# Reordering the projections of an RWKV-7 layer, moving its bonus product, and regrouping modulation and start-up loads

## The chip, the cores and the metric

The kernel runs on one core of one Trainium2 chip. The metric is the device time of one launch in microseconds (us). Three runs of the kernel before gave a median of 3932.47 us (3931.03 to 3934.02). The profile is of a fourth execution that took 3921.72 us.

## The reference, cut to what matters

The model has one RWKV-7 layer and one attention layer, each with a SwiGLU part, on 1024 prompt tokens and 8 x 16 sample tokens of width 1024, in float32. Only the first layer's mixing and the modulations matter here:

```
mod = silu(c) @ w_ada + b_ada                      # shift, scale, gate of each sublayer
h = rmsnorm(x) * (1 + scale) + shift;  xx = h_prev - h
xr, xw, xk, xv, xa, xg = h + xx * mix[0..5]
r, k, v = xr @ w_r, xk @ w_k, xv @ w_v
decay from sigmoid(w0 + tanh(xw @ w1) @ w2);  a = sigmoid(a0 + (xa @ a1) @ a2)
g = sigmoid(xg @ g1) @ g2                          # g1 is 1024 x 160: g1a 128 wide, g1b 32 wide
y, state = wkv7(r, decay, k, v, -kk, kk * a)       # a recurrence over tokens
y = groupnorm(y) * ln_w + ln_b + sum(r * k * r_k) * v    # the bonus
out = (y * g) @ w_o
```

## The kernel before, in words

**Arithmetic.** Most products split both operands into a high and a low float32r part and add three matmuls (`mm3`, line 257; `split`, line 253, is one ScalarE copy and one VectorE subtraction). A few small products are plain float32.

**Stages of the first layer.** The 1152 tokens are three blocks of 384 (`proj`, line 462). A block's projections are: `proj_h` (norm and modulation of h), the low-rank stage `proj_lora` (line 511: three first products wa1, g1a, g1b from the split h, then 24 second products of one or two short matmuls each, for w2, a2 and g2), `proj_k`, `proj_r`, `proj_v`, each eight output tiles (f) of 24 matmuls of 128 x 384. `mixed` (line 418) makes the 16 token-mixed tiles of an operand; they live in a ring `mix` of 17 slots, so the next operand's tiles come free as the last product of the one before consumes its own. Results go to DRAM (`spill`, `save`) and are read back by the recurrence.

**The recurrence.** A block has three windows of 128 tokens in two halves: six units. `inverses` (line 717) makes the small triangular inverses of a block's windows from the spilled kk and b: `win_first`, a solve on VectorE (`win_solve`, lines 792 to 796), four merge steps (`win_merge`), with DRAM round trips between. `win_prep` (line 729) loads and masks a unit's operands (rings XL, YL, BKT of three slots), `win_run` carries the state through the unit, `win_post` (line 962) normalises and gates. `windows` (line 1032) prepares two units ahead. Units of block b - 1 are alternated with the projections of block b, five steps to four (line 1100).

**The last stretch.** After the third block's projections the last six units (in the order 12, 13, 16, 14, 15, 17 of line 1113) alternate with `early`: 32 modulation steps, then the output projections of blocks 0 and 1; block 2's follows the units. Then come the SwiGLU part (its down projection carries the other 16 modulation units, `step(7)` in `begin`, line 1291) and the second layer.

**Modulations.** `ada_steps` (line 194): a unit of 512 columns has four loads of 512 KB, each followed by two plain float32 matmuls into two of four 32-row quarters of a bank, then a copy, four small matmuls and a bias add. The first four units are needed before the first block's h; their loads share the ring `raw` of three slots.

**What sets the order.** The building framework reorders each engine's instructions at build time: the order of the code is a priority, and what its own model of time holds ready, with a free slot, goes first. On the chip each engine and each DMA queue then keeps that fixed order.

Of the kernel before, what the change touches and what calls it, by code (L numbers as in the profile page):

```python
# [8 lines left out]
F32 = mybir.dt.float32  # L9
# [7 lines left out]
NB = 3  # L17
# [8 lines left out]
def _cst():  # L26
# [24 lines left out]
    add("qs", (p % 32)[:, None] == np.arange(16)[None, :])  # L51
    add("cen", np.eye(128) - (p[:, None] // 64 == p[None, :] // 64) / 64.0)
# [24 lines left out]
def prep(i):  # L77
# [38 lines left out]
    d["g2a"], d["g2b"] = g2[:128], np.concatenate([g2[128:]] * 3, 0)  # L116
# [24 lines left out]
class Trunk:  # L141
# [52 lines left out]
    def ada_steps(self, units, tag="aux", bufs=1):  # L194

        nc = self.nc
        for u in units:
            ps = self.bank(tag, bufs)
            for kp in range(4):
                w = self.rawtile()  # L200
                nc.sync.dma_start(w[:, :1024], self.a["wada"][u, kp])
                for j in range(2):
                    k = 2 * kp + j
                    q = 32 * (k % 4)
                    mm(nc, ps[q:q + 32, :], self.scT[:, k, :], w[:, j * 512:(j + 1) * 512], k < 4, k >= 4)
                if kp < 3:
                    yield
            sb = self.rawtile()[:, :512]
# [130 lines left out]
    def proj_open(self, ctx):  # L339
# [3 lines left out]
        self.nmix, self.nmr = 17, 2  # L343
# [8 lines left out]
    def lora_weights(self):  # L352

        nc, pp = self.nc, self.pp
        self.lw = {}
        for n, mixes, w in (("wa1", (1, 4), 64), ("g1a", (5,), 128), ("g1b", (5,), 32)):
            c = 8 * w * len(mixes)
            raw = pp.tile([128, 1024], F32, tag="raw", name=self.nm("raw"), bufs=self.nraw)
            nc.sync.dma_start(raw[:, :c], self.a[n])
            m = pp.tile([128, 1024], F32, tag="raw", name=self.nm("raw"), bufs=self.nraw)  # L360
            for j, i in enumerate(mixes):
                v = lambda t: t[:, :c].rearrange("p (k j w) -> p j k w", j=len(mixes), w=w)[:, j]
                nc.vector.tensor_tensor(v(m), v(raw), self.P(f"mix{i}").rearrange("p (k o) -> p k o", o=1).broadcast_to([128, 8, w]),
                                        ALU.mult)
            nc.vector.tensor_tensor(raw[:, :c], raw[:, :c], m[:, :c], ALU.subtract)
            self.lw[n] = []
            for t in (raw, m):
# [4 lines left out]
    def proj_h(self, b):  # L372
# [15 lines left out]
        for f in range(8):  # L388
            x = hb[:, f]
            if b == 0:  # L390
                if f % 4 == 0:
                    self.step(8)
# [69 lines left out]
    def proj(self, b):  # L462
# [17 lines left out]
        if b + 1 < NB:  # L480
            self.x = self.hsplit()
# [1378 lines left out]
```

## Time and profile before

| | |
|---|---|
| median of three runs | 3932.47 us |
| the profiled execution | 3921.72 us, span 3919.9 us |
| TensorE (PE) busy | 3594.0 us, 92% of the span, granted clock 0.928 on average |
| VectorE (DVE) busy | 2273.5 us, 58% |
| ScalarE (ACT) busy | 1588.3 us, 41% |
| GpSimd (POOL) busy | 632.7 us, 16% |
| DMA queue of SyncE (q1) | 375728 packets, 530.77 MB, 43.0% of 16 engines' span |
| chain that ended last | PE 64%, DMA 6%, DVE 5%, ACT 3% |

In the page's 40 slices (98 us each) PE is at 5 to 9 tenths and the clock at 6 to 9 tenths in the first 14 slices, that is, in the first layer's mixing; after that both are at 9 in nearly all slices. A busy TensorE is not TensorE at its peak: at a granted clock of 0.5 it is busy for twice as long with the same work.

### The profile page before, as it was taken

To read this page: it belongs to the slowest core of one execution; us is meant where nothing else is said; L and a number is where in the kernel's file an instruction comes from. 1 tells how busy PE (TensorE), PEld (TensorE's weight loads), DVE (VectorE), ACT (ScalarE), POOL (GpSimd) and SP (SyncE) were. 2 spreads that over 40 slices of the span, in tenths; PEclk is the share of its full clock that TensorE was granted. 3 is DMA by queue.
4 is the path that set the end of the run, shared out by engine and by line. 5 is a ranking of instruction groups with operands and counts; after the bars stand their busy time and mean duration, and the time that the engine had idled before them with its cause. 6 is when DMAs were issued, how large, how long until landed. Compare 5 with 4: busy or idle time off the path is not lost.

```text
span 3919.9 us, 71529 instructions
## 1 busy us (share of the span) xinstructions
PE 3594.0 (92%) x28214; PEld 3116.0 (79%) x28214; DVE 2273.5 (58%) x4259; ACT 1588.3 (41%) x2993; POOL 632.7 (16%) x569
## 2 busy tenths in 40 slices
PE   5788989999899789999999999898888799999999
PEld 3676777777568579999877888777677799999998
DVE  3667566564435765555355852566676765454567
ACT  4654546554223443333311254455554443333310
POOL 0000000000000265445000200100000365454000
PEclk8787889799689789999999999999999899999999
DMA  6774676576656422222655213255464422222522
GB/s 205 223 233 130 208 223 173 160 229 193 176 148 195 136 88 74 74 76 74 225 204 186 92 61 103 81 171 153 145 203 150 148 72 74 76 71 94 171 81 73
DMA packets 430208, 554.22 MB, mean 141 GB/s; under 512 B 128528, under 2 KB 297872, under 8 KB 425392
## 3 DMA queue, kind: packets, MB, share of 16 engines
q1 hardware_dynamic: 375728, 530.77, 43.0%
q10 hardware_dynamic: 54144, 18.89, 2.1%
q8 instruction: 222, 3.64, 0.4%
q14 instruction: 114, 0.93, 0.1%
HBM read 415.39 MB, written 134.12 MB: 140 GB/s over the span
## 4 chain that ended last, share of the span: by engine, by line
PE 64%; DMA 6%; DVE 5%; ACT 3%; issue 2%; POOL 1%; SPq 1%; ACTq 0%; DVEq 0%; POOLq 0%
PE S L138 31%; PE PT L138 15%; PE acc L138 8%; PE st L138 3%; PE O L138 2%; DVE h L255 1%; PE PT L1686 1%; PE aux L138 1%; PE G L138 1%; PE Y L138 1%; DMA rr<-sf_cs 1%; DMA mr<-yg 1%; ACT pts L1687 0%; ACT h L254 0%; DMA yg<-y 0%
## 5 line engine op out<-in xcount | busy, mean ns | idle before, releaser
L138 PE MATMUL S<-h,w 128*128 128x320 f32 (+1 forms) x4944 | 694.7, 299 | 17.8 <-DVE h L255 5.7
L138 PEld LDWEIGHTS S<-h,w 128*128 128x128 f32 x4944 | 674.8, 192 | 25.5 <-DVE h L255 10.0
L138 PE MATMUL acc<-mx,whi 128*128 128x384 f32 (+1 forms) x1824 | 527.0, 367 | 57.9 <-ACT whi L254 19.0
L138 PE MATMUL S<-h,wh 128*128 128x320 f32 (+1 forms) x2844 | 528.9, 337 | 13.5 <-DVE h L1056 8.1
L138 PEld LDWEIGHTS S<-h,wh 128*128 128x128 f32 x2844 | 454.4, 189 | 82.5 <-DVE h L1312 12.6
L138 PEld LDWEIGHTS acc<-mx,whi 128*128 128x128 f32 (+1 forms) x1824 | 344.1, 197 | 95.8 <-ACT whi L254 23.9
L254 ACT ACTIVATE w<-rq 128x512 fp32r<-128x512 f32 x308 | 192.0, 629 | 501.6 <-PE S L138 199.8
L255 DVE TENSOR_TENSOR w<-rq,w 128x512 fp32r<-128x512 f32 x308 | 271.4, 885 | 198.2 <-ACT w L254 197.5
L138 PE MATMUL PT<-h,w 128*128 128x320 f32 (+1 forms) x2448 | 353.3, 299 | 14.0 <-ACT w L254 6.4
L138 PEld LDWEIGHTS PT<-h,w 128*128 128x128 f32 x2448 | 335.7, 191 | 18.3 <-ACT w L254 6.8
L138 PE MATMUL acc<-mx,wlo 128*128 128x384 f32 (+1 forms) x912 | 328.3, 361 | 3.2 <-DVE wlo L255 3.2
L138 PE MATMUL PT<-h,wh 128*128 128x320 f32 (+1 forms) x1428 | 286.7, 344 | 6.7 <-DVE wh L255 3.9
L1245 POOL TENSOR_TENSOR t<-t,t 128x576 f32<-128x576 f32 (+1 forms) x132 | 215.0, 1629 | 412.4 <-ACT t L1252 296.0
L138 PEld LDWEIGHTS PT<-h,wh 128*128 128x128 f32 x1428 | 234.6, 191 | 42.0 <-DVE h L1312 6.9
L255 DVE TENSOR_TENSOR wlo<-raw,whi 128x1024 fp32r<-128x1024 f32 (+1 forms) x123 | 145.2, 1181 | 90.6 <-ACT whi L254 88.9
L138 PEld LDWEIGHTS acc<-mx,wlo 128*128 128x128 f32 (+1 forms) x912 | 179.5, 197 | 15.1 <-DVE wlo L255 5.9
L254 ACT ACTIVATE whi<-raw 128x1024 fp32r<-128x1024 f32 (+1 forms) x123 | 125.6, 1023 | 118.4 <-PE acc L138 93.4
L255 DVE TENSOR_TENSOR h<-h,h 128x1024 fp32r<-128x1024 f32 (+4 forms) x112 | 122.9, 1112 | 81.8 <-ACT h L254 67.3
L254 ACT ACTIVATE wh<-rq 128x512 fp32r<-128x512 f32 x124 | 74.6, 626 | 231.2 <-PE S L138 144.2
L254 ACT ACTIVATE h<-h 128x1024 fp32r<-128x1024 f32 (+4 forms) x112 | 103.2, 935 | 157.2 <-DMA h<-sd 113.4
L1312 DVE TENSOR_TENSOR h<-h,S 128x640 f32<-128x640 f32 (+1 forms) x150 | 112.1, 752 | 92.3 <-PE S L138 92.0
L1245 DVE TENSOR_TENSOR t<-S,t 128x576 f32<-128x576 f32 (+1 forms) x116 | 86.5, 745 | 132.7 <-PE S L138 132.5
(399 smaller groups left out, 5744.4 us busy)
## 6 DMA issues: line engine op xcount, KB each, us to landing
h<-in_wada SPq DMA_DIRECT2D x64, 512.0 KB, 6.1
raw<-in_wada SPq DMA_DIRECT2D x48, 512.0 KB, 4.4
rq<-in_wg SPq DMA_DIRECT2D x88, 256.0 KB, 2.6
rq<-in_wu SPq DMA_DIRECT2D x88, 256.0 KB, 2.6
rq<-in_wd SPq DMA_DIRECT2D x88, 256.0 KB, 3.0
kc<-in_ck SPq DMA_DIRECT2D x16, 1024.0 KB, 5.1
vc<-in_cv SPq DMA_DIRECT2D x16, 1024.0 KB, 5.9
sd<-t SPq DMA_DIRECT2D x88, 160.0 KB, 1.9
```

Source lines behind the costliest of these rows:

```text
L138: return nc.tensor.matmul(out, lhsT, rhs, start=start, stop=stop)
L254: self.nc.scalar.activation(hi, x, AF.Copy)
L255: self.nc.vector.tensor_tensor(lo, x, hi, ALU.subtract)
L1245: eng.tensor_tensor(out, x, y, ALU.add)
L1312: nc.vector.tensor_tensor(y, y, d, ALU.add)
L1686: nc.tensor.transpose(pt[:, j * 128:(j + 1) * 128], P[:, j * 128:(j + 1) * 128], self.C("ident"))
```

## The change

It reorders a block's projections to: first low-rank products, then v woven one to three with the second low-rank products, then k, the next block's h, and r with the inverses. It makes g1b a plain float32 product in four quarters, keeps the first block's low-rank weights in SBUF, does the bonus product per unit on GpSimd, moves two products of `proj_k` to GpSimd, regroups the modulations by four, gives the first modulation loads eight other tiles, shortens three rings of the recurrence from three to two and its look-ahead from two units to one. The core of the diff:

```diff
-    def ada_steps(self, units, tag="aux", bufs=1):
+    def ada_steps(self, units, tag="aux", bufs=1, tile=None):
...
-            for kp in range(4):
-                w = self.rawtile()
-                nc.sync.dma_start(w[:, :1024], self.a["wada"][u, kp])
-                for j in range(2):
-                    k = 2 * kp + j
-                    q = 32 * (k % 4)
-                    mm(nc, ps[q:q + 32, :], self.scT[:, k, :], w[:, j * 512:(j + 1) * 512], k < 4, k >= 4)
-                if kp < 3:
+            for h in range(2):
+                w = [(tile or self.rawtile)() for _ in range(2)]
+                for i in range(2):
+                    nc.sync.dma_start(w[i][:, :1024], self.a["wada"][u, 2 * h + i])
+                for q in range(4):
+                    mm(nc, ps[32 * q:32 * q + 32, :], self.scT[:, 4 * h + q, :], w[q // 2][:, q % 2 * 512:q % 2 * 512 + 512],
+                       h == 0, h == 1)
+                if h == 0:
                     yield
...
-        self.nmix, self.nmr = 17, 2
+        self.nmix, self.nmr = 18, 2
...
+    def lora_in(self, n):
+        c = 8 * self.LORA[n][1] * len(self.LORA[n][0])
+        if n not in self.lw:
+            ts = self.lora_weights(n)
+        else:
+            ts = [self.rawtile() for _ in range(2)]
+            for t, d in zip(ts, self.lw[n]):
+                self.nc.sync.dma_start(t[:, :c], d)
+        if n == "g1b":
+            return ts
...
     def proj(self, b):
         if b == 0:
-            self.ada = self.ada_steps((0, 2, 1, 3), "acc", 2)
+            self.lw = {}
+            ring = (f() for _ in range(3) for f in self.early)
+            self.ada = self.ada_steps((0, 2, 1, 3), "acc", 2, lambda: next(ring))
...
-            self.lora_weights()
...
-        x, k = self.x, self.mixed(2, b)
-        yield from self.proj_lora(b, *x)
+        x, v = self.x, self.mixed(3, b)
+        second = self.proj_lora(b, *x)
+        for _ in range(3):
+            yield next(second)
+        k = self.mixed(2, b)
+        yield from self.alternate(second, self.proj_v(b, *v), 3, 1)
         r = self.mixed(0, b)
         yield from self.proj_k(b, *k)
-        v = self.mixed(3, b)
-        yield from self.alternate(self.inverses(b), self.proj_r(b, *r))
         if b + 1 < NB:
             self.proj_h(b + 1)
-        yield from self.proj_v(b, *v)
-        if b + 1 < NB:
             self.x = self.hsplit()
+        yield from self.alternate(self.inverses(b), self.proj_r(b, *r))
...
-            self.save("bn", b, f, bn)
+            self.spill("bn", b, f, bn)
...
+        def narrow(n):
+            pw = self.bank("acc", 2)
+            W = self.lora_in(n)
+            for i in range(2):
+                for k in range(8):
+                    q = 32 * (k % 4)
+                    mm(nc, pw[q:q + 32, :TB], W[i][:, k * 32:k * 32 + 32], self.hgroups(self.hb[:, k])[i],
+                       i == 0 and k < 4, i == 1 and k >= 4)
+            u = self.ev("kk")
+            nc.scalar.activation(u, pw[:, :TB], AF.Copy)
+            mm(nc, pw[0:32, :TB], self.C("q4"), u, True, True)
+            return pw
...
-        pg = first("g1b", 32)
+        pg = narrow("g1b")
...
-            vv = self.ev("vv", 2)
-            self.load(vv, "bn", b, f)
             v = self.ev("e0", 4)
             nc.scalar.activation(v, pz[:, :TB], AF.Copy)
-            nc.vector.tensor_tensor(vv, vv, pz[:, :TB], ALU.mult)
-            nc.scalar.activation(vv, vv, AF.Identity, bias=self.P("lnb", f))
-            self.spill("v", b, f, vv)
+            self.spill("v", b, f, v)
...
-            nc.vector.tensor_tensor(ag, ag, iv, ALU.mult)
+            nc.gpsimd.tensor_tensor(ag, ag, iv, ALU.mult)
             self.spill("b", b, f, ag)
-            nc.vector.tensor_tensor(iv, iv, kp, ALU.mult)
+            nc.gpsimd.tensor_tensor(iv, iv, kp, ALU.mult)
...
+        self.early = [lambda: flat(self.wt("YL", [128, 2, 2, 4, 64], 2))] * 2 + \
...
-        ring, nr = (self.st, 1) if (w, hf) == (7, 1) and 1 else (self.wt, 3)
+        ring, nr = (self.st, 1) if (w, hf) == (7, 1) and 1 else (self.wt, 2)
...
+        bn = self.wt("bn", [128, 512], 1)
+        nc.sync.dma_start(bn.rearrange("p (f t) -> p f t", f=4), self.sp[b]["bn"][:, wi, fs, :])
+        nc.gpsimd.tensor_tensor(bv, bv, bn, ALU.mult)
...
-        nc.vector.tensor_tensor(y, y, gt, ALU.mult)
+        for f in range(4):
+            s = slice(f * 128, (f + 1) * 128)
+            nc.vector.scalar_tensor_tensor(y[:, s], y[:, s], self.P("lnb", 4 * hf + f), gt[:, s], ALU.add, ALU.mult)
...
-        n = 2
+        n = 1
...
-            for _ in range(32):
+            for _ in range(16):
...
-            self.step(7)
+            self.step(3)
```

## Rows read from the trace of the kernel before

**Rows 1.** Stretches: length, PE, PEld, DVE, ACT, POOL busy us, clock, DMA share, GB/s.
```profile
0.00:66.00 66.00, 25.94 (x99) 7.28 (x99) 22.43 (x54) 26.40 (x44) 1.29 (x8) 0.87 0.72 247
318.00:650.00 332.00, 298.39 (x3304) 246.59 (x3305) 214.99 (x472) 181.47 (x347) 4.89 (x19) 0.87 0.66 186
1006.00:1170.00 164.00, 143.16 (x1640) 94.53 (x1639) 68.57 (x179) 36.57 (x77) 0.00 (x0) 0.73 0.59 170
90.00:137.00 47.00, 40.25 (x130) 25.74 (x129) 23.63 (x33) 32.26 (x57) 0.19 (x1) 0.71 0.61 194
365.00:425.00 60.00, 52.99 (x636) 40.16 (x635) 33.76 (x64) 32.35 (x64) 0.29 (x1) 0.60 0.54 154
650.00:740.00 90.00, 83.55 (x808) 61.35 (x806) 54.12 (x114) 57.85 (x99) 0.00 (x0) 0.74 0.51 150
1890.00:2200.00 310.00, 310.00 (x1754) 238.59 (x1753) 166.46 (x258) 67.17 (x94) 4.60 (x3) 1.00 0.55 194
```

**Rows 2.** Timeline of the start: start us, us, engine, line, what, count, idle before.
```profile
17.49 26.37 SPq L201 DMA_DIRECT2D raw<-in_wada  x13
...
47.83 1.05 PE L138 MATMUL acc<-raw,scT 128*32 128x512 f32 x4 [0.22 <-DMA raw<-in_wada]
...
57.04 0.07 DVE L402 MEMSET hb<- 128x8 f32 x1
...
59.31 2.06 DVE L255 TENSOR_TENSOR mx<-hb,mx 128x408 fp32r<-128x408 f32 x4
...
61.74 14.91 SPq L247 DMA_DIRECT2D raw<-lw  x6
...
66.51 1.01 PE L138 MATMUL acc<-mx,whi 128*128 128x384 f32 x2 [15.86 <-ACT whi L254]
```

**Rows 3.** Timeline of PE in g1b's product of block 0.
```profile
88.72 0.34 PE L138 MATMUL acc<-mx,wlo 128*32 128x384 f32 x1
...
89.26 0.34 PE L138 MATMUL acc<-mx,wlo 128*32 128x384 f32 x1
```

**Rows 4.** Timeline of PE around modulation matmuls.
```profile
944.75 1.06 PE L138 MATMUL aux<-raw,scT 128*32 128x512 f32 x8
945.74 0.69 PE L138 MATMUL st<-t,Aab 32*32 32x32 f32 x16
```

**Rows 5.** Groups on PE in the down projection, 1890 to 2200 us.
```profile
L138 PE MATMUL acc<-h,scT 128*32 128x512 f32 x256 | 54.3, 603 | 0.0
```

**Rows 6.** Groups in the second low-rank products of block 0, 90 to 137 us.
```profile
L534 ACT ACTIVATE e<-acc,par 128x384 f32<-128x384 f32 x16 | 9.2, 575 | 3.7 <-DMA sf_cs<-e 1.9 <-PE acc L138 1.8
...
L254 ACT ACTIVATE whi<-raw 128x1024 fp32r<-128x1024 f32 x6 | 6.3, 1054 | 3.0 <-PE acc L138 3.0
L427 ACT ACTIVATE mr<-hb,om 128x384 f32<-128x384 f32 x8 | 4.9, 609 | 2.2 <-DVE mx L255 2.1
```

**Rows 7.** Groups of POOL over the span, and of DVE from 1400 to 1890 us.
```profile
L1219 POOL TENSOR_TENSOR rq<-rq,rq 128x512 f32<-128x512 f32 x42 | 54.3, 1293 | 24.8 <-DMA sd<-t 17.7 <-POOL rq L1218 6.8
...
L1259 DVE TENSOR_TENSOR t<-t,t 128x576 f32<-128x576 f32 (+1 forms) x21 | 35.0, 1666 | 25.0 <-POOL t L1245 25.0
...
L1261 DVE TENSOR_TENSOR t<-t,t 128x576 f32<-128x576 f32 (+1 forms) x21 | 16.5, 785 | 0.0
```

**Rows 8.** Timeline marks of the last block: k, last solve, a unit's preparation, last residual.
```profile
821.51 0.91 PE L138 MATMUL aux<-sq,cst 128*128 128x384 f32 x2 [0.20 <-ACT sq L640]
...
983.57 0.39 DVE L796 TENSOR_REDUCE T<-stmp 128x15 f32<-128x225 f32 x1
...
1069.12 0.61 SPq L742 DMA_DIRECT2D BK<-sp_b  x1
...
1072.01 0.39 DVE L796 TENSOR_REDUCE T<-stmp 128x15 f32<-128x225 f32 x1
...
1084.36 0.60 ACT L774 ACTIVATE BKT<-G 128x512 f32<-128x512 f32 x1
...
1373.67 0.48 DVE L1056 SCALAR_TENSOR_TENSOR e<-acc,mod,rr 128x256 f32<-128x256 f32 x1 [1.64 <-PE acc L138]
```

More of the change, by code (lines that the diff above doesn't have):

```diff
@@ L350, in hgroups @@
         return v[:, :, 1:17], v[:, :, 0:16]
[L352 to L367, printed above, removed]
-                dt = self.dp.tile([128, c], F32, name=self.nm("lw"))
-                nc.scalar.dma_start(dt, t[:, :c])
-                self.lw[n].append(dt)
+    LORA = {"wa1": ((1, 4), 64), "g1a": ((5,), 128), "g1b": ((5,), 32)}
@@ new lines, in lora_weights @@
+    def lora_weights(self, n):
+        nc = self.nc
+        mixes, w = self.LORA[n]
+        c = 8 * w * len(mixes)
+        raw, m = self.rawtile(), self.rawtile()
+        nc.sync.dma_start(raw[:, :c], self.a[n])
+        for j, i in enumerate(mixes):
+            v = lambda t: t[:, :c].rearrange("p (k j w) -> p j k w", j=len(mixes), w=w)[:, j]
+            nc.vector.tensor_tensor(v(m), v(raw), self.P(f"mix{i}").rearrange("p (k o) -> p k o", o=1).broadcast_to([128, 8, w]),
+                                    ALU.mult)
+        nc.vector.tensor_tensor(raw[:, :c], raw[:, :c], m[:, :c], ALU.subtract)
+        self.lw[n] = []
+        for t in (raw, m):
+            dt = self.dp.tile([128, c], F32, name=self.nm("lw"))
+            nc.scalar.dma_start(dt, t[:, :c])
+            self.lw[n].append(dt)
+        return raw, m
@@ new lines, in lora_in @@
+    def lora_in(self, n):
[8 more added lines that the diff above has]
+            return ts
+        W = []
+        for t in ts:
+            hi = self.pp.tile([128, 1024], F32R, tag="whi", name=self.nm("whi"), bufs=self.nhi)
+            lo = self.pp.tile([128, 1024], F32R, tag="wlo", name=self.nm("wlo"), bufs=self.nlo)
+            self.split(hi, lo, t)
+            W.append((hi, lo))
+        return W
@@ L537, in second @@
                 self.save(spill, b, f, sg)
-                if f % 4 == 3:
-                    yield
-            self.last_sg = ins
-        pw = first("wa1", 128)
+                self.last_sg = ins
+                yield
+        pw = first("wa1")
         yield
@@ L550, in proj_lora @@
         self.split(ta[0:64], ta[64:128], th[:64])
-        pg = first("g1a", 128)
+        pg = first("g1a")
         yield
@@ L593, in proj_v @@
             self.gemm(pz[:, :TB], W, hi, lo)
[L594 removed]
+            if b == 2 and f % 2:
                 self.step(1)
[L596 to L597 removed]
             v = self.ev("e0", 4)
             nc.scalar.activation(v, pz[:, :TB], AF.Copy)
[L600 to L602 removed]
+            self.spill("v", b, f, v)
             pt = self.bank("aux", 1)
```

55 lines of the change are left out of this document (33 added, 22 removed).

## The prediction

> **What bounds the kernel now.** I read the page's slices first: they say where TensorE is short of work, namely only in the first layer's mixing. Then I cut that part into stretches and looked at busy time and granted clock side by side [rows 1]. In 318 to 650 us TensorE is busy for 298.39 of 332 us at a clock of 0.87: it is the bound, yet a tenth of the stretch is idle and more is lost to the lower clock level (1.2 instead of 2.4 GHz). The loss of a stretch is idle time plus busy time times (1 - clock). It gathers in three stretches in which the 24 second low-rank products run: 90 to 137 us (6.75 idle + 40.25 x 0.29 = 18.4 us), 365 to 425 us (7.0 + 21.2 = 28.2 us) and 650 to 740 us (6.45 + 21.7 = 28.2 us), and in the last stretch, 1006 to 1170 us (20.8 + 38.7 = 59.5 us). At the start TensorE waits until 66.51 us for its first split weight [rows 2]. In the down projection it is busy for 310.00 of 310 us at a clock of 1.00 [rows 1]: there every microsecond of matmul counts.
>
> **The change part by part.**
>
> *Start.* The last modulation load is used at 47.83 us, h is done at 57.04 us, and the low-rank weights then go to DRAM and back (issued at 61.74 us) before the first product at 66.51 us [rows 2]. The new order keeps them in SBUF and can prepare them before h is done: after 57.04 us one split remains, an ACT copy and a DVE subtraction of about 0.52 us each (2.06 us for four [rows 2]), so the first product can start near 58.5 us: -8 us. Eight tiles instead of three let more of the 13 later loads fly. The stretch moves 247 GB/s at a DMA share of 0.72 [rows 1]; it could gain up to 0.28 of the 26 us of issuing, 7 us, or nothing if 1.1 MB of low-rank weights is now loaded beside them. I take -3 us. Sum -11 us (-5 to -15). The eight tiles belong to the recurrence, whose first units run hundreds of microseconds later, so nothing waits there.
>
> *g1b.* 48 matmuls per block, three each 0.54 us [rows 3], are 8.6 us. The new form is 16 float32 matmuls in four groups of four. Four such matmuls (eight records) hold TensorE for 0.99 us at 512 columns, from 944.75 to the next instruction at 945.74, while a pair alone (four records) takes 1.05 us (at 47.83 us [rows 2]): matmuls in different quarters run side by side. At 384 columns that is 0.74 us a group, 3.0 us, plus the summing matmul (at most 0.91 us, the nearest float32 product [rows 8]). 8.6 - 3.9 = 4.7 us a block, -14 us in all. The copy between (0.6 us by the ACT row of that size [rows 6]) is a new wait, covered by the w2 products behind it, which need only the first product.
>
> *Weaving v with the second products.* TensorE's second products (64 matmuls of 0.18 us [rows 3], 11.5 us) are joined by v's 192 (34.6 us): 46 us per block. ACT in the same stretch has 24 evacuations of 0.575 us, 11 weight splits of 1.054 us, eight mixings of 0.609 us with a copy of about 0.5 us after each, and v's 16 copies of about 0.5 us [rows 6]: 13.8 + 11.6 + 8.9 + 8 = 42 us; DVE has less (23.63 us to ACT's 32.26 in the first of these stretches [rows 1]). So TensorE becomes the bound there, just. The three lossy stretches hold 18.4 + 28.2 + 28.2 = 74.8 us. All of it is the upper bound of the gain; the lower is a loss of about 15 us, because the rings now change operands v to k with no other products behind (eight mixings, 9 us of ACT, partly under the last v product), three times 5 us. I take 60%, -45 us, nearer the upper end because the ACT sum stays under TensorE's.
>
> *Last stretch.* It has half as many modulation steps before the output projections of blocks 0 and 1, which are dense work for the idle 20.8 us and the 0.73 clock [rows 1]. Bounds: all of the 59.5 us, and nothing, if the units' chain sets the end. I take a third, -20 us, since the inverses below are now late.
>
> *Modulations in the down projection.* 256 records hold TensorE for 54.3 us [rows 5]; as 32 groups of four at 0.99 us [rows 4] they hold it for 31.7 us: -22 us, nothing hides it there. If the groups come apart because the second load is late, 0.
>
> *Bonus, GpSimd, rings.* The bonus adds a load and a GpSimd product per unit and three more DVE instructions at its end, and takes a load, a DVE and an ACT instruction from v. The products of b and k move to GpSimd: 48 of about 1.0 us (1.293 us at 512 columns [rows 7], by columns). Their spills wait that much longer in SyncE's queue, and the weight loads behind them with them; loads are issued a tile ahead, so I take 0 to 10 us. With rings of two and one unit of look-ahead a unit's preparation (15 us, from its BK load at 1069.12 to its copy at 1084.36 [rows 8]) can start only when the last but one unit is through; between blocks other products cover that. Together +9 us (-5 to +30).
>
> DVE's instructions with two SBUF inputs slow down beside GpSimd: 1666 ns for those at line 1259, which start as GpSimd works, against 785 ns for the same shape at line 1261 [rows 7]. The Trainium skill ("SBUF — State Buffer", Who interferes with whom) says that such an instruction and a GpSimd one that reads SBUF exclude each other for the whole instruction; the trace agrees, and the rule gives the third rival below.
>
> Sum: -11 - 14 - 45 - 20 - 22 + 9 = -103 us on the profiled execution's 3921.72 us. It is 10.75 us under the median of the runs, which I keep as an offset: 3932.47 - 103 = 3829 us.
>
> **The rivals.**
>
> *The last block's chain decides.* From the last k product at 821.51 us to the last residual at 1373.67 us is 552 us [rows 8], with three solves in series before the units that need them. v now stands ahead of k, so k's end moves back by v's 34.6 us, 44 us at the utilisation of such a stretch (298.39 x 0.87 / 332 = 0.78 [rows 1]), against the 70 us saved before it by the start, g1b and weaving; no v product is left to run beside the inverses, and the 552 us stay. Then only -26 and the down projection's -22 remain: 3884 us. For it: the last two solves end 88 us apart, at 983.57 and 1072.01 us [rows 8], far more than a solve takes. Against: their steps then had v products ahead of them in TensorE's queue, and the output projections can fill the gap.
>
> *The look-ahead is missed.* All 18 units have their preparation, up to 15 us, exposed instead of beside the unit before. It decides from 103 / 18 = 5.7 us a unit; at 8 us the time is 3829 + 144 = 3973 us, slower. For it: the loads of a unit were slot-bound already (BK has one slot). Against: TensorE has other products in two of three blocks.
>
> *GpSimd holds DVE.* Each of the 48 products blocks DVE for its 1.0 us and frees 0.55 us; if DVE were the bound in k's stretch, +22 us: 3851 us, still faster. Against: DVE is busy for 215 of 332 us [rows 1].
>
> *The regrouping does not happen.* If the float32 matmuls are issued in pairs as before, the down projection gains nothing: 3851 us.
>
> **How the numbers follow.** My forecast with its near variants (the last two rivals among them): 0.64. The chain decides: 0.19. Look-ahead missed: 0.12. The remaining 0.05: gains and losses cancel. About 0.2% (8 us) is what a measurement can tell from no change. Faster by more than that: 0.64 + 0.19 = 0.83, less 0.01 for the chain's far end: 0.82. Same: 0.05. Slower: 0.13. The range goes from -152 us (start -15, g1b -14, nearly all of the weaving -71, half of the last stretch -30, down projection -22, nothing lost) to -14 us, which takes in the chain's case: 3780 to 3918 us; most of the slower case is left out.
>
> **What would show it.** Right: first split product near 55 us; clock near 0.9 or more where the second products and v now run together; 32 groups of eight records in the down projection and that stretch shorter by 20 us or so; the last residual of the mixing at about 1290 us instead of 1374. Wrong: a clock of 0.5 to 0.7 again in the woven stretches, TensorE waiting for `mx` at the change from v to k, a last stretch in which TensorE waits for TT or for BK, or DVE instructions of k's stretch at twice their time.

## The result and the profile after

The changed kernel takes **3939.14 us** (median of 18 runs, 3929.76 to 3946.69) against 3930.61 us of the kernel before on the same chip (18 runs): ratio 1.0023, 95% interval 1.0015 to 1.0032. It is slower by 0.2%, where 3829 us was forecast. The profiled execution has a span of 3940.1 us, 20.2 us more than that of before.

From its page: the span, the engines' busy time, and TensorE's busy tenths and clock in 40 slices.

```profile
span 3940.1 us, 71465 instructions
PE 3559.0 (90%) x28172; PEld 3107.7 (79%) x28172; DVE 2265.0 (57%) x4238; ACT 1574.5 (40%) x2967; POOL 712.4 (18%) x635
PE   6878988888798789999999999888889799999999
PEclk8888998799689689999999999999999899999999
```

TensorE is busy for 35 us less than before in a span that is 20.2 us longer, so it is idle for 55 us more. The marks of the changed kernel that answer to [rows 2] and [rows 8], from its timeline (first split product; last product of `proj_k` of block 2; last step of block 2's last solve; last residual of the mixing):

```profile
51.55 0.69 PE L139 MATMUL acc<-mx,whi 128*128 128x384 f32 x1 [3.96 <-ACT mx L255]
...
866.27 0.81 PE L139 MATMUL aux<-sq,cst 128*128 128x384 f32 x2
...
1109.05 0.39 DVE L842 TENSOR_REDUCE T<-stmp 128x15 f32<-128x225 f32 x1
...
1388.31 0.48 DVE L1107 SCALAR_TENSOR_TENSOR e<-acc,mod,rr 128x256 f32<-128x256 f32 x1 [2.00 <-PE acc L139]
```

Against before, the first split product comes 15 us earlier (66.51), the last k product 44.8 us later (821.51), the last solve 37.0 us later (1072.01), and the mixing ends 14.6 us later (1373.67). The other 5.6 us of the span's difference lie behind the mixing. From the mixing's end to the end of the span the twenty profiled executions (both kernels and all experiments below) take between 2546 and 2566 us, the kernel before the least of all; in the second layer alone, whose code is the same in all, they scatter by 18 us. So a difference of ten or twenty microseconds between two single executions need not come from the edit.

Stretches of the changed kernel, columns as in [rows 1]: the first three stretches of those rows, then the three in which v is now woven with the second products, and the last:

```profile
0.00:66.00 66.00, 35.27 (x163) 21.38 (x164) 29.06 (x61) 31.80 (x52) 1.28 (x8) 0.84 0.65 239
318.00:650.00 332.00, 289.59 (x3004) 239.99 (x3005) 217.47 (x461) 182.93 (x342) 29.67 (x39) 0.90 0.66 189
1006.00:1170.00 164.00, 136.76 (x1671) 99.78 (x1671) 77.15 (x194) 43.10 (x83) 4.28 (x2) 0.75 0.62 173
...
78.00:150.00 72.00, 57.84 (x260) 50.19 (x261) 27.20 (x31) 37.85 (x67) 0.00 (x0) 0.86 0.67 199
310.00:430.00 120.00, 99.32 (x1195) 83.31 (x1196) 68.02 (x156) 54.63 (x105) 0.00 (x0) 0.83 0.60 165
610.00:800.00 190.00, 161.09 (x1977) 130.77 (x1974) 102.34 (x232) 92.56 (x169) 2.91 (x4) 0.78 0.60 168
946.00:1100.00 154.00, 117.17 (x1589) 74.54 (x1589) 62.47 (x189) 33.95 (x73) 3.80 (x3) 0.67 0.71 204
```

By the forecast's own formula (idle plus busy times one less the clock) the woven stretches lose 14.2 + 8.1, 20.7 + 16.9 and 28.9 + 35.4 us, 124 us together. The three stretches of before lost 74.8 us; these are longer, 382 us against 197, since they hold v's products too, but those were to fill the loss. The clock there is 0.86, 0.83 and 0.78, where 0.9 or more was to be the sign of being right. In the same three windows the kernel before, with partly other work in them, loses 22 + 43 + 42 = 107 us:

```profile
78.00:150.00 72.00, 63.39 (x243) 46.45 (x243) 36.21 (x53) 43.26 (x75) 0.85 (x4) 0.79 0.56 177
310.00:430.00 120.00, 104.50 (x1328) 82.97 (x1329) 68.06 (x148) 60.58 (x119) 0.29 (x1) 0.74 0.51 140
610.00:800.00 190.00, 175.81 (x1870) 142.66 (x1867) 128.81 (x292) 114.18 (x212) 5.94 (x22) 0.84 0.60 167
```

In the last stretch of the changed kernel, 946 to 1100 us, TensorE is idle for 36.8 us and the clock's mean is 0.67, between its two levels of 1.2 and 2.4 GHz.

What TensorE waits for in the third woven stretch (groups of PE from 610 to 800 us; idle before the group and releasers at the end):

```profile
L139 PE MATMUL st<-t,Aab 16*32 16x16 f32 (+1 forms) x544 | 15.7, 203 | 5.5 <-DVE t L862 5.1 <-ACT xs L924 0.4
...
L139 PE MATMUL acc<-ag,l2h 128*128 128x384 f32 x16 | 7.8, 485 | 10.8 <-ACT e L641 4.8 <-ACT e L579 4.4 <-ACT kp L604 1.5
...
L645 PE MATMUL aux<-cst,e 128*128 128x128 f32 x24 | 5.0, 326 | 5.0 <-ACT e L641 4.6 <-DVE mod L216 0.4
```

The second products wait for ScalarE's copies out of v's banks (L641) as well as for their own (L579), v's transposes wait for the same copies, and the merges of block 1's inverses (`st<-t,Aab`) now run here with 544 of their 576 records. Before, 192 of them ran ahead of 650 us, beside that block's r and v.

### The profile page after: what moved, and what is told of

It reads as the page before. It is cut to its first block, busy times and chain, and to the rows that moved or that the text cites. A ratio compares the mean times of both kernels' runs of the same rounds, so it can differ in the third digit from the quotient of the medians.

```text
span 3940.1 us, 71465 instructions
## 1 busy us (share of the span) xinstructions
PE 3559.0 (90%) x28172; PEld 3107.7 (79%) x28172; DVE 2265.0 (57%) x4238; ACT 1574.5 (40%) x2967; POOL 712.4 (18%) x635
## 4 chain that ended last, share of the span: by engine, by line
PE 61%; DMA 6%; DVE 5%; ACT 3%; POOL 2%; issue 1%; SPq 0%; ACTq 0%; DVEq 0%; POOLq 0%
PE S L139 31%; PE PT L139 15%; PE acc L139 7%; PE st L139 2%; PE O L139 2%; DVE h L256 1%; PE PT L1737 1%; PE aux L139 1%; PE Y L139 1%; PE G L139 1%; DMA raw<-in_wada 1%; ACT pts L1738 1%; DMA h<-qT 0%; DMA h<-out_kT 0%; DMA h<-in_wq 0%
## 5 line engine op out<-in xcount | busy, mean ns | idle before, releaser
L139 PE MATMUL acc<-mx,whi 128*128 128x384 f32 x1728 | 525.6, 383 | 49.2 <-ACT mx L255 20.2
L139 PEld LDWEIGHTS acc<-mx,whi 128*128 128x128 f32 x1728 | 355.7, 214 | 77.6 <-ACT mx L255 23.3
L139 PE MATMUL acc<-mx,wlo 128*128 128x384 f32 x864 | 325.7, 377 | 2.4 <-DVE wlo L256 2.4
L139 PEld LDWEIGHTS acc<-mx,wlo 128*128 128x128 f32 x864 | 184.0, 213 | 10.0 <-DVE wlo L256 3.7
L256 DVE TENSOR_TENSOR wlo<-raw,whi 128x1024 fp32r<-128x1024 f32 x108 | 136.7, 1267 | 94.7 <-ACT whi L255 93.5
L255 ACT ACTIVATE whi<-raw 128x1024 fp32r<-128x1024 f32 x108 | 113.5, 1053 | 104.5 <-PE acc L139 78.9
```

Of the source, the lines that this page charges most:

```text
L139: return nc.tensor.matmul(out, lhsT, rhs, start=start, stop=stop)
L255: self.nc.scalar.activation(hi, x, AF.Copy)
L256: self.nc.vector.tensor_tensor(lo, x, hi, ALU.subtract)
```

## The experiments

Each time is a median, each ratio (with its 95% interval) is to the kernel before, run in the same job; "the changed kernel" is 3939 us throughout. The median of the kernel before lies between 3930.61 and 3936.36 us from job to job, so kernels of different jobs are compared by their ratios too. Marks in microseconds are from one profiled execution of each kernel.

**The last block in the old order.** Block 2 alone gets the order of before, with the low-rank stage's yields thinned to the old number.

```diff
+        if b + 1 == NB:
+            x, k = self.x, self.mixed(2, b)
+            for i, _ in enumerate(self.proj_lora(b, *x)):
+                if i < 3 or i % 4 == 2:
+                    yield
+            r = self.mixed(0, b)
+            yield from self.proj_k(b, *k)
+            v = self.mixed(3, b)
+            yield from self.alternate(self.inverses(b), self.proj_r(b, *r))
+            yield from self.proj_v(b, *v)
+            return
```

> The last block alone goes back to the order of before (k right after the low-rank stage, r with the inverses, v last); blocks 0 and 1 stay in the new order. If the last block's chain from k to the inverses sets the end (chain theory), k of the last block ends 40 to 50 us earlier than in the changed kernel (at about 820 us instead of 866), its solves follow, and the time falls to about 3885 us. If the shorter look-ahead of the windows costs what the projections gained (look-ahead theory), the time stays within 10 us of the changed kernel's 3939 us.

3983.72 us, ratio 1.0116 (1.0081 to 1.0151). Block 2's k was done 76 us earlier, and yet the last residual came at 1418.6 us. Block 1's last solve ended at 825 us instead of 767, block 2's at 1134 instead of 1109; neither theory foresaw that, and no run shows its cause. The last block's own k, the rival of the prediction, doesn't decide.

**The ratio of steps.** `self.alternate(w, self.proj(b), 5, 4)` becomes `5, 6`.

> The new order everywhere, but the windows get five steps to six of the projections instead of five to four, so that the inverses no longer stand behind some 34 window steps (21 before the change). Chain theory: the first solve of the last block, 971 us in the changed kernel with k ended at 866 us, comes 40 us or more earlier, and the time falls by 20 to 50 us to 3890 to 3920 us. If only the place of v ahead of k matters, the first solve stays about 100 us behind k and the time within 10 us of 3939 us. Look-ahead theory: no gain or a loss.

3936.22 us, 1.0001 (0.9980 to 1.0021). The first solve of block 2 ended 59 us earlier (923 us), as the chain theory said, and so did the last solves of blocks 1 and 2 (739 and 1056 us instead of 767 and 1109); the units of blocks 0 and 1 ended 68 and 50 us later. The time fell by 3 us, not by 20 to 50: the inverses came earlier and nearly nothing was gained.

**Two units ahead, rings of two.** `n = 1` becomes `n = 2` in `windows`.

> The changed kernel with windows prepared two units ahead again in the order of the code; the rings stay at two slots (three do not fit beside the new tiles). Look-ahead theory: 3939 us falls by 30 us or more. Chain theory: within 10 us of 3939 us, or slower, since more window steps stand before the inverses.

4022.96 us, 1.0217 (1.0185 to 1.0250), 84 us more than the changed kernel, the opposite of the look-ahead theory. I take it that with rings of two the second unit's slots are not free and what needs them waits; that was not tried.

**The old pairs of modulations**, with the old counts of `step`.

> The changed kernel with the modulations in pairs of matmuls and one load at a time, as before, with the old counts of steps. If the regrouping never formed groups of four in the down projection (TensorE held 51.1 us by them before, 49.3 us after), the time stays within 8 us of 3939 us. If it paid and the loss is elsewhere, it rises by about 20 us to 3960 us. If twice the loads at once hurt, it falls.

3950.59 us, 1.0034 (1.0018 to 1.0050); the interval overlaps that of the changed kernel. The down projection took as long with either: from the last silu of the SwiGLU part to its last residual 372.4 us with the pairs, 371.1 us in the changed kernel and 372.6 us in the kernel before. The changed kernel's modulation matmuls there, two runs of them from the timeline:

```profile
1913.34 1.92 PE L139 MATMUL acc<-h,scT 128*32 128x512 f32 x16
1924.54 1.05 PE L139 MATMUL acc<-h,scT 128*32 128x512 f32 x4
```

and their group from 1890 to 2220 us:

```profile
L139 PE MATMUL acc<-h,scT 128*32 128x512 f32 x244 | 50.5, 602 | 0.5 <-DMA h<-in_wada 0.5
```

Where 16 records stand together they hold TensorE for 0.96 us per eight, as [rows 4] said; but a run of four takes 1.05 us, and 33 of the changed kernel's 44 runs are of two, four or six. The kernel before has 45 runs, and 138 of its 256 records already stand in runs of eight or more; in the changed kernel 130 do. The regrouping hardly changed the groups. Taking overlaps out, all records hold TensorE for 52.4 us instead of 54.3.

**The inverses' bank from acc.** In `win_first`, `self.bank("G", 2)` becomes `self.bank("acc", 2)`.

> Edit of the changed kernel: the first products of the inverses (win_first) take their PSUM bank from acc (2 banks) instead of G (2 banks), so that they no longer share banks with the preparation of the windows. G-bank theory (the shared banks put the inverses of a block and the preparations of the block before in one series, and this series ends the mixing whatever the projections do): the first copy of block 1's inverses (Aab) moves from 580 us to about 530 us, that of block 2 from 943 us to about 890 us, the last residual of the mixing from 1388 us to 1340 to 1370 us, and the time falls by 20 to 50 us, to about 3890 to 3920 us. Rival (the units themselves, with a look-ahead of one, set the end; the inverses only wait because the order of the build puts them late): less than 8 us of difference, 3931 to 3947 us.

3975.64 us, 1.0113 (1.0087 to 1.0139). It doesn't test what it was to test: the acc banks go round in the order of the code too, so that block 1's first low-rank product now stands behind block 0's last inverses (its tanh moves from 299 to 364 us). The split further below does it better.

**The old order in all blocks**, the rest of the change kept:

```diff
-        x, v = self.x, self.mixed(3, b)
-        second = self.proj_lora(b, *x)
-        for _ in range(3):
-            yield next(second)
-        k = self.mixed(2, b)
-        yield from self.alternate(second, self.proj_v(b, *v), 3, 1)
+        x, k = self.x, self.mixed(2, b)
+        for i, _ in enumerate(self.proj_lora(b, *x)):
+            if i < 3 or i % 4 == 2:
+                yield
         r = self.mixed(0, b)
         yield from self.proj_k(b, *k)
+        v = self.mixed(3, b)
+        yield from self.alternate(self.inverses(b), self.proj_r(b, *r))
         if b + 1 < NB:
             self.proj_h(b + 1)
+        yield from self.proj_v(b, *v)
+        if b + 1 < NB:
             self.x = self.hsplit()
-        yield from self.alternate(self.inverses(b), self.proj_r(b, *r))
```

> Edit of the changed kernel: all three blocks have the order of before (second low-rank products, k, r with the inverses, v last), with the yields of the low-rank stage thinned to the old number; everything else of the change stays (start, g1b, bonus, GpSimd, rings, look-ahead, modulations in fours). If weaving v with the second products has its forecast gain of 45 us and something else loses it, this kernel takes 3975 to 3990 us. If the new order is what gives its gain back through a longer chain behind k and the inverses, this kernel is faster than the changed one: 3890 to 3920 us. If order and chain balance, 3931 to 3947 us. The look-ahead theory says that it stays above the kernel before by 10 us or more.

**3897.24 us, 0.9912 (0.9889 to 0.9935): faster than both kernels.** So the order costs 42 us (44 by the ratios), and the rest of the change brings 36 (3932.76 us for before in this job). Its marks: end of block 0's k and last solve, end of block 2's k and last solve, last residual.

```profile
167.82 0.91 PE L139 MATMUL aux<-sq,cst 128*128 128x384 f32 x2 [1.13 <-ACT sq L681]
356.41 0.39 DVE L843 TENSOR_REDUCE T<-stmp 128x15 f32<-128x225 f32 x1
769.76 0.91 PE L139 MATMUL aux<-sq,cst 128*128 128x384 f32 x2 [1.68 <-ACT sq L681]
1030.18 0.39 DVE L843 TENSOR_REDUCE T<-stmp 128x15 f32<-128x225 f32 x1
1335.42 0.48 DVE L1108 SCALAR_TENSOR_TENSOR e<-acc,mod,rr 128x256 f32<-128x256 f32 x1 [1.51 <-PE acc L139]
```

Block 2's k is done 96.5 us before that of the changed kernel, its last solve 78.9 us, the last residual 52.9 us.

**One unit ahead in the kernel before**: its three rings of three become two, `n = 2` becomes `n = 1`, nothing else.

> Edit of the kernel before: only the rings XL, YL and BKT of the recurrence go from three slots to two and its look-ahead from two units to one; the order of the projections and all else stay as before. Look-ahead theory (a unit's preparation is exposed once the ring is shorter): the time rises by 30 us or more, to 3960 us or more, and the six last units end later than 1374 us by as much. G-bank theory (the preparations stand in one series with the inverses, whatever the look-ahead): between -10 and +10 us, 3920 to 3940 us.

3921.96 us, 0.9968 (0.9949 to 0.9986). The shorter look-ahead and rings gain 11 us by themselves, 5 to 20 by the interval; the look-ahead theory is wrong.

**The two products of `proj_k` on VectorE again**: `nc.gpsimd.tensor_tensor` becomes `nc.vector.tensor_tensor` in two lines of the changed kernel.

> Edit of the changed kernel: the two products of proj_k (b and k) run on VectorE again instead of GpSimd. GpSimd theory (VectorE is held by GpSimd, and the spills behind the products are late, which delays the inverses): 10 to 25 us faster, 3914 to 3929 us. Rival (VectorE has slack there and the inverses wait for banks): less than 8 us either way, 3931 to 3947 us.

3937.57 us, 1.0015 (0.9997 to 1.0032): nothing. Yet VectorE is held, as one group of `proj_k` shows, first in the kernel before:

```profile
L655 DVE SCALAR_TENSOR_TENSOR kk<-kk,ext 128x384 f32<-128x384 f32 (+2 forms) x32 | 13.9, 451 | 1.2 <-DVE ag L652 0.5
```

then in the changed one,

```profile
L695 DVE SCALAR_TENSOR_TENSOR kk<-kk,ext 128x384 f32<-128x384 f32 (+2 forms) x32 | 23.1, 740 | 1.0
```

and with the products back on VectorE:

```profile
L695 DVE SCALAR_TENSOR_TENSOR kk<-kk,ext 128x384 f32<-128x384 f32 (+2 forms) x32 | 14.7, 479 | 1.1
```

The instruction beside the products rises from 451 to 740 ns and falls back to 479; the 9 us of all 32 are not on the path.

**The new order in one block only.** The same edit as for the old order, under `if b != 0:`, `if b != 1:` or `if b != 2:`.

> Edit of the changed kernel: only block 0 keeps the new order (v woven with the second products, then k, then r with the inverses); blocks 1 and 2 have the order of before. Place theory (v ahead of k costs time because k, r and the inverses of a block come later, and only where the inverses are what the units wait for, which block 0's are not, since its units have all of block 1's projections to run beside): the time of the kernel with the old order in all blocks or a little less, 3882 to 3900 us. Rival (the woven stretch itself is slow, by about the same in each block): a third of the 42 us that lie between the two orders is lost, 3905 to 3917 us.

> Edit of the changed kernel: only block 1 keeps the new order; blocks 0 and 2 have the order of before. Cover theory (with v gone ahead, a block's inverses run on after its r products and meet the k of the next block if that one begins in the old order; the last block in the old order behind a woven block 1 took 3984 us): slower than the changed kernel, 3945 to 3990 us, with block 1's last solve after 790 us. Place theory alone (each block's own k is late by v's time, and only the last block's decides): 3890 to 3915 us. Even-share rival: 3905 to 3917 us.

> Edit of the changed kernel: only block 2 keeps the new order; blocks 0 and 1 have the order of before. Place theory: the last block's k ends at 820 to 865 us instead of 769 us, its last solve at 1065 to 1110 instead of 1030 us, the last residual 35 to 60 us later than 1335 us, and the time is 3930 to 3960 us, that is, all that the new order costs. Even-share rival: 3905 to 3917 us. If block 2's order does not matter, 3890 to 3904 us.

Block 0 only: 3933.52 us, 0.9995 (0.9984 to 1.0006). Block 1 only: 3917.73 us, 0.9948 (0.9933 to 0.9962). Block 2 only: 3910.95 us, 0.9922 (0.9900 to 0.9944). Over the old order's 3897 that is 36, 20 and 14 us (33, 14 and 4 by the ratios; the interval of the last overlaps that of the old order). The place theory foresaw the opposite, nothing in block 0 and all in block 2; the cover theory's loss with block 1 alone did not come either; and the three don't add up to the 42 us of all together. With block 2 alone in the new order its k ends 97 us later than in the old order (866 for 770 us) and the mixing only 18 us later (1353.8 for 1335.4). With block 0 alone in the new order its k, its last solve, block 2's last solve and the last residual are:

```profile
213.93 1.65 PE L139 MATMUL aux<-sq,cst 128*128 128x384 f32 x2 [3.48 <-ACT sq L695]
408.92 0.39 DVE L857 TENSOR_REDUCE T<-stmp 128x15 f32<-128x225 f32 x1
1085.16 0.39 DVE L857 TENSOR_REDUCE T<-stmp 128x15 f32<-128x225 f32 x1
1374.11 0.48 DVE L1122 SCALAR_TENSOR_TENSOR e<-acc,mod,rr 128x256 f32<-128x256 f32 x1 [1.45 <-PE acc L139]
```

Against the old order k is late by 46.1 us, the last solve of block 0 by 52.5, that of block 2 by 55.0, the end by 38.7. The projections catch up (block 1's k is late by 9.3 us, block 2's by 23.3), the inverses don't: the last solves of the three blocks are late by 52.5, 52.4 and 55.0 us. A delay made in the first 210 us is carried a thousand microseconds on, in the inverses and not in the projections.

**v ahead of k, not woven.**

```diff
-        yield from self.alternate(second, self.proj_v(b, *v), 3, 1)
+        for g, n in ((second, 6), (self.proj_v(b, *v), 2)):
+            for i, _ in enumerate(g):
+                if i % n == n - 1:
+                    yield
```

> Edit of the changed kernel: v stays ahead of k in all blocks, but its products come after all second low-rank products instead of one to three among them (the number of steps of the recurrence beside them stays the same). It prices the weaving at a fixed place of v. If weaving has its forecast gain of 45 us, 3984 us. If it gains about what the first block showed (the projections of block 0 end 13 us earlier than in the old order) and nothing in the others, 3945 to 3960 us. If weaving itself loses, below 3930 us.

3921.39 us, 0.9958 (0.9943 to 0.9972): 18 us less than woven (26 by the ratios, and the intervals are apart). At this place of v, weaving loses, where 45 us were to be gained. So 18 of the order's 42 us are the weaving's, and 24 come with v's place ahead of k.

**One bank each for the inverses and the preparations**, in the changed kernel and in the one with the old order. `win_first` takes `self.bank("Gi", 1)`; in `win_prep` each of the two banks of a pair is filled and read before the next is taken:

```diff
-            Gs = [self.bank("G", 2) for _ in range(2)]
-            for f in range(4):
-                for e in range(2):
+            for e in range(2):
+                G = self.bank("G", 1)
+                for f in range(4):
```

> Edit of the changed kernel: of the two PSUM banks that the inverses' first products and the windows' preparations share, one goes to each (the preparation then makes its four banks of results one after the other). Bank theory: the first copy of block 1's inverses moves from 580 us to 545 us or earlier, that of block 2 from 943 to 910 us or earlier, and the time falls to 3895 to 3925 us. Rival (the units and their order set the end): the copies move by less than 10 us and the time stays at 3930 to 3950 us, or rises because a preparation with one bank takes longer.

> Edit of the kernel with the old order in all blocks (everything else as changed): the same split of the two banks. Bank theory: first copies of the inverses of blocks 1 and 2 at 465 us or earlier and 830 us or earlier (480 and 851 us there), time 3865 to 3888 us. Rival: 3890 to 3910 us.

3956.94 us, 1.0055 (1.0038 to 1.0072), and 3912.96 us, 0.9946 (0.9932 to 0.9961): 18 and 16 us more than without (in the old order the intervals overlap a little). First copies of block 1's and block 2's inverses, the last solve's end and the last residual, in the changed kernel with the split:

```profile
499.10 0.59 ACT L758 ACTIVATE Aab<-Gi 128x512 f32<-128x512 f32 x1
837.14 0.60 ACT L758 ACTIVATE Aab<-Gi 128x512 f32<-128x512 f32 x1
1161.44 0.38 DVE L840 TENSOR_REDUCE T<-stmp 128x15 f32<-128x225 f32 x1
1389.70 0.48 DVE L1105 SCALAR_TENSOR_TENSOR e<-acc,mod,rr 128x256 f32<-128x256 f32 x1 [1.66 <-PE acc L139]
```

In the changed kernel itself:

```profile
579.27 0.58 ACT L758 ACTIVATE Aab<-G 128x512 f32<-128x512 f32 x1
942.56 0.60 ACT L758 ACTIVATE Aab<-G 128x512 f32<-128x512 f32 x1
```

The copies come 80 and 105 us earlier, as the bank theory said; the last solve comes 52 us later (1161 for 1109), and the mixing still ends within 1.4 us of where it did (1389.70 for 1388.31; this profiled execution, 3945.54 us, is the fastest of its kernel). The banks decide when the inverses begin, not when they end; and the last solve doesn't set the end of the mixing.

**Five steps to five, old order**: `5, 4` becomes `5, 5`.

> Edit of the kernel with the old order in all blocks: five steps of the recurrence alternate with five of the projections instead of four, so that a block's inverses stand ahead of more of the preparations of the block before. Bank theory: first copy of block 1's inverses before 465 us, last solve of block 1 before 695 us, of block 2 before 1010 us, time 3872 to 3888 us. Rival (units set the end): the units of blocks 0 and 1 end later by what the inverses win, 3890 to 3910 us.

3911.00 us, 0.9938 (0.9915 to 0.9961): the last solves of blocks 1 and 2 come 20 and 31 us earlier (693 and 1000 us), the last output of block 0's units is sent 39 us later (716 instead of 677 us), and nothing is gained, as the rival said: 14 us more, with intervals that overlap.

**Two thirds of v's products left out, old order.** `self.gemm` in `proj_v` becomes eight matmuls of the high parts:

```diff
-            self.gemm(pz[:, :TB], W, hi, lo)
+            for q in range(8):
+                mm(self.nc, pz[:, :TB], W[0][:, q * 128:(q + 1) * 128], hi[q], q == 0, q == 7)
```

> Edit of the kernel with the old order in all blocks: of the three products of each split matmul of v only the first is made, in all blocks, which leaves 384 matmuls of 0.18 us, 69 us of TensorE's work, out. If TensorE's total work bounds the mixing, the time falls by 69 us or more, to 3828 us or less. If a series of inverses and units sets its end, v is beside it and the time falls by less than half of that, to 3862 to 3897 us.

**3910.21 us, 0.9932 (0.9912 to 0.9952): no faster with 384 matmuls less.** It is 13 us more than with all of them (8 by the ratios, with intervals that overlap), above both forecast ranges. The mixing from 66 to 1330 us, columns as in [rows 1], with all of v's products (old order):

```profile
66.00:1330.00 1264.00, 1091.53 (x11095) 879.89 (x11094) 755.20 (x1590) 592.92 (x1115) 118.63 (x147) 0.86 0.66 190
```

and with a third of them:

```profile
66.00:1330.00 1264.00, 1054.11 (x10650) 825.66 (x10649) 736.50 (x1568) 587.28 (x1107) 114.94 (x147) 0.82 0.65 188
```

Busy time at full clock falls from 1091.53 x 0.86 = 939 to 1054.11 x 0.82 = 864 us, by 74. Idle time rises by 37.4 us (172.5 to 209.9) and the time lost to the lower clock by 36.9 (152.8 to 189.7). In a window of fixed length the two must make up for the work taken out; the rows show that they share it evenly, and the last residual shows that the end came no earlier (1348.5 us for 1335.4). In the old order TensorE's work doesn't bound the mixing.

**Block 0's k earlier, old order.** In block 0, `proj_lora` is called in two parts: w2 and a2 with their first product before k; g1a, g1b and g2 after r, from a second split of h.

```diff
+            for i, _ in enumerate(self.proj_lora(b, *x, part=0)):
...
+            yield from self.proj_k(b, *k)
+            x = self.hsplit()
+            def rg():
+                yield from self.proj_r(b, *r)
+                for i, _ in enumerate(self.proj_lora(b, *x, part=1)):
...
+            yield from self.alternate(self.inverses(b), rg())
```

> Edit of the kernel with the old order in all blocks: in block 0 alone the gate's low-rank products (g1a, g1b, g2) are made after r, from a second split of h, so that k comes right after the second products of w2 and a2. Series theory (the mixing ends about 1170 us after block 0's k, so what moves that end forward moves the end of the mixing): k of block 0 ends at 140 to 155 us instead of 167 us, the last residual 8 to 25 us before 1335 us, time 3872 to 3889 us. Rival (the end of block 0's k only goes along with it, and the later blocks set the end): the second split and the moved products cost 5 to 10 us and give nothing, 3897 to 3910 us.

3915.36 us, 0.9951 (0.9936 to 0.9966). Block 0's k and last solve, and the last residual:

```profile
149.32 0.91 PE L139 MATMUL aux<-sq,cst 128*128 128x384 f32 x2 [0.59 <-ACT sq L706]
358.24 0.39 DVE L868 TENSOR_REDUCE T<-stmp 128x15 f32<-128x225 f32 x1
1362.15 0.48 DVE L1133 SCALAR_TENSOR_TENSOR e<-acc,mod,rr 128x256 f32<-128x256 f32 x1 [1.61 <-PE acc L139]
```

k ends 18.5 us earlier, the block's first two solves 12.0 and 8.3 us earlier, its last 1.8 us later. But the gate's products now stand between r and v, and block 1's k ends 29 us later (478 for 449 us); the time is above both ranges. So an earlier k doesn't bring the end forward if it is bought in this way; an earlier k by itself was not tried.

**The solves cut**, in the changed kernel: `for i in range(1, 16)` in `win_solve` becomes `range(1, 2)`.

> Edit of the changed kernel: each of the nine solves makes only the first of its fifteen rows, so that 28 of its 30 VectorE instructions are left out and its result is not the inverse. Series theory with the inverses as a link (each solve takes 11 to 23 us from its first to its last instruction, three in series in each block): the last solves of blocks 0, 1 and 2 end 20 to 40 us earlier each against the block before, and the time falls by 40 to 90 us, to 3850 to 3900 us. Rival (the six units of a block, not the inverses, pace the mixing, or the build's order does): within 20 us of the changed kernel, 3920 to 3960 us.

3928.34 us, 0.9979 (0.9958 to 1.0001): 11 us less than the changed kernel (17 by the ratios), though VectorE has 9 x 8 us less to do and nine links of the supposed series are shorter. The end of the last solve and the last residual:

```profile
1052.53 0.15 DVE L842 TENSOR_REDUCE T<-stmp 128x1 f32<-128x1 f32 x1
1374.97 0.48 DVE L1107 SCALAR_TENSOR_TENSOR e<-acc,mod,rr 128x256 f32<-128x256 f32 x1 [1.45 <-PE acc L139]
```

The last solves of the three blocks end 39, 45 and 57 us earlier than in the changed kernel, as the series theory said, and the mixing ends only 13 us earlier. The k of blocks 1 and 2 end 40 and 35 us later. The rival's bounds hold it; the solves are at most a small link.

**What the end of the mixing goes by.** The last send of a unit's output, in the changed kernel and in the one with the old order:

```profile
1329.39 0.37 ACTq L1038 DMA_DIRECT2D yg<-y  x1
1277.29 0.37 ACTq L1039 DMA_DIRECT2D yg<-y  x1
```

In all twenty traces the last residual comes 58 to 61 us after this send, whether the mixing ends at 1335 or at 1459 us. From the end of the last solve to the last residual it is 228 us (banks split) to 348 us (old order, five to five). So the mixing ends when the last unit ends, and the last solve says little of it.

## Why the prediction was wrong, point by point

**The step that failed is the weaving, -45 us.** It read idle time and low clock of three stretches as time that denser work would give back. With two thirds of v's products taken away, in the old order, the time did not fall: this time was slack, and the mixing ends when the last unit of the recurrence ends. The order costs 42 us with all blocks and 36 with block 0 alone; at a fixed place of v the weaving itself loses 18 us, where 45 were to be gained. The bound I gave on the bad side, a loss of 15 us from the change of operands, priced the wrong thing; so the range ended 21 us below the result. Together the order's 42 us lost and the 36 us that the rest brings give +6 us, near the 8.5 us measured. The ground for calling TensorE the bound was 298.39 busy of 332 us [rows 1]. The Trainium skill ("Trainium Kernel Development and Optimization", Performance Expectations) says that matmul busy time is a bad measure of how close a kernel is to its roofline, because matmuls are pipelined. These runs bear the warning out for another reason, work that nothing waits for: 74 us of it gone and no time won.

**The last stretch, -20 us,** did not come: 1006 to 1170 us loses 27.2 + 34.2 = 61.4 us, where it lost 59.5. From the last output of block 1's units to the last of block 2's it is 305 us, against 278 before and 277 with the old order. So halving the modulation steps, each of which now holds twice the matmuls, made it no shorter even where the inverses are not late; what paces it is not shown.

**The start, -11 us,** was right in kind and a little small: 15 us, at the end of its bounds. **g1b, -14 us,** was not tried alone. In the traces its matmuls hold TensorE for 8.8 to 9.0 us a block before and 3.5 to 4.9 us in the changed kernel, with 0.8 to 1.0 us for the summing product: 12 us in all, so its work was sized well; what it is worth in time is open. The old order in all blocks beats the kernel before with one unit ahead by 3921.96 - 3897.24 = 24.7 us; start and g1b were put at 25 together, but this difference holds the modulations, the bonus and GpSimd's products too and single edits scatter by half as much (below), so it does not show the sum right.

**Modulations, -22 us:** the rival "the regrouping does not happen" came true, and the down projection is as long as before. The premise was off as well: the 54.3 us of [rows 5] were not the price of pairs, since 138 of the 256 records already stood in runs of eight or more.

**Bonus, GpSimd, rings, +9 us:** the sign was wrong as far as it was tried. Rings of two with one unit ahead gain 11 us in the kernel before; the products on GpSimd cost nothing that can be measured; the bonus was not tried alone. The rival "look-ahead missed" falls with it. "GpSimd holds DVE" is true of the instructions (451 to 740 ns, where the Trainium skill, "SBUF — State Buffer", Who interferes with whom, has such an instruction wait), and worth nothing in time.

**The rival "the last block's chain decides"** came nearest in kind, though its 3884 us is 55 us too low, from k's end moved back by v's 44 us and 70 us saved before it. k's end moved by 44.8 us net, so the 70 us were not there; the old order in all blocks has its k 51.7 us earlier than before, without any weaving. But the chain is not the last block's alone: with that block in the old order the kernel took 3984 us, and with that block alone in the new order k came 97 us later and the end of the mixing 18.

**What stays open** is what paces the units, and so the cause of the order's 42 us. Excluded as sole cause: TensorE's work (in the old order), the last block's k, the shared banks, the solves' instructions, the end of the last solve. All five kernels with the old order in all blocks take 3897 to 3915 us, and the best of them is the one that nothing was done to, even when work was taken out; the changed kernel and four small edits of it (ratio of steps, products on VectorE, pairs of modulations, banks split) take 3936 to 3957. The gap between the groups is the order's; v not woven (3921) and the solves cut (3928) lie between. Differences of 13 to 18 us within a group I can't put on a mechanism. A part is scatter behind the mixing: with the pairs of modulations the mixing ends as in the changed kernel (1388.8 and 1388.3 us), and 11 us more pass in the second layer. That the build fixes another order of all queues for each edit would explain the rest; it was not shown.

## What to carry to other kernels

Before pricing idle time of a busy engine as a gain, take some of its work out and see whether the time falls: here 74 us of matmuls less made nothing faster, and one such run would have warned that weaving had little to win. In a mix of dense work and a recurrence, try first the order that makes what the recurrence waits for and keeps the dense work that nothing waits for behind it, beside the recurrence's own steps: here it was 42 us faster. Where a build tool reorders everything, judge an order by several near versions of it, not by one.

## What the runs showed of the hardware that was not expected

In the same 1264 us, with 445 matmul records fewer, TensorE's mean granted clock fell from 0.86 to 0.82, between its two levels of 1.2 and 2.4 GHz. So its busy time fell by only 37.4 us (1091.53 to 1054.11), where its work at full clock fell by 74. A VectorE instruction with two inputs in SBUF took 740 ns instead of 451 beside GpSimd's products, and the kernel's time did not move.
